# Tiles on SBUF's left side moved 96 bytes against the tiles on its right side

## The chip, the cores and the metric

The kernel runs on one core of a Trainium2 chip. The core has a matrix engine (TensorE, PE in the profile, whose weight loads have a row of their own, PEld), a vector engine (DVE), a scalar engine (ACT), GpSimd (POOL), a queue engine that issues transfers (SP), and 16 DMA engines that move data between DRAM and the on-chip memory SBUF. SBUF has 128 partitions; a tile takes the same byte range in each of them, and "address" below means the byte offset within a partition. The metric is the time of one execution in microseconds on the device, taken as the median of several runs.

## What is computed

One residual block on 512 tokens of width 1024, all in float32. The reference, cut to its shape:

```python
h = rms_norm(x, norm1_g)
proj = h @ w_in          # q,k,v of branch A | q,k,v of branch B | gates gA, gB
out_a = chunked_attention(qa, ka, va, q_norm_g, k_norm_g, rel_bias)  # 8 heads x 64
out_b = stick_breaking_attention(qb, kb, vb)                         # 8 heads x 64
mixed = sigmoid(gA) * (out_a @ w_branch_a) + sigmoid(gB) * (out_b @ w_branch_b)
x = x + mixed @ w_out
hid = causal_conv3(rms_norm(x, norm2_g) @ w_ffn_up) + conv_b         # 2 x 2816 wide
x = x + (silu(hid[gate]) * hid[up]) @ w_ffn_down
```

## The kernel before

Every float32 product is made of three TensorE products. A number is split into a high part that TensorE takes exactly (`hi`, type fp32r) and the rest (`lo`), and `mm3` issues hi*hi, hi*lo and lo*hi into one PSUM bank. ACT makes the high part by a copy, DVE the low part by a subtraction. The activations after each norm are kept so in two tiles, `hth` and `htl` (128 x 8 x 512). The weights come from DRAM in chunks of 128 x 2048 into `raw`, and are split into `whi` and `wlo`, two buffers of each.

A matmul has two operands in SBUF. The stationary one (128 x 128) is loaded into the array by a weight load (PEld); the moving one (128 x 256 or 128 x 512) is streamed past it. The weight load of the next matmul runs beside the matmul before it. In a row of the profile such as `pg<-hth,whi_up 128x512` the two tiles stand behind the arrow, in the order of the names or not; the text says which is which.

The stages in order of time, and the operands of their matmuls:

- 0 to about 53 us: `uA`, `vA` (L433, L439): `hth`/`htl` stationary, `whi`/`wlo` moving, mostly 512 wide.
- 50 to 315 us: the two attentions, with fill-in projections between their steps: `qA`, `kA`, `vB` (`hth`/`htl` stationary, weights moving, 256 wide), `gA`, `qkB`, `gB` (weights stationary, `hth`/`htl` moving, 512 wide), `yA` (weights stationary, attention outputs `oh`/`ol` moving, 512 wide).
- 315 to 382 us: `yB` and the output projection `wo` (weights with attention outputs, or with `mh`/`ml`), then the second norm, which writes `hth`/`htl` anew.
- 382 to 612 us: the up projection. `up0`, `up1` 256 wide and the plain `up` chunks 512 wide have weights stationary and `hth`/`htl` moving (L300 to L302). Twelve chunks use a seven-product scheme (L1169), 256 wide: three of its seven products move `hth`/`htl`, four move sums of them, `ts`.
- 612 to 722 us: the down projection (L1269): the pair tiles `ax`, `ay` are stationary, `whi_dn`/`wlo_dn` moving, 512 wide.

SBUF is filled from two ends. The pools made without `side="right"` grow from the low end: `sm` (the parameters' tile `par`), `wp` (`raw`, `whi`, `wlo`), and then the pools of the attention stages (`cp`, `pv`, `pst`, `pqn`, `ppt`, `pwk`, `po`, `pc`, `ppk`), which later give their place to the pool `fp` of the feed-forward part. The pool `hp` (side="right") holds `hth` and `htl` at the high end; for the down projection `hp2` takes its place and holds `ax9`, `ay9`, `ax10`, `ay10`, one `raw` and two `t2` tiles.

The addresses that the built program gives to some of these tiles, with the remainder by 64 and by 256:

| tile | pool, side | address | mod 64 | mod 256 |
|---|---|---|---|---|
| par | sm, left | 1152 | 0 | 128 |
| whi, wlo (two each) | wp, left | 18304, 26752, 35200, 43648 | 0 | 128 |
| v (first) | pv, left | 68480 | 0 | 128 |
| ax1 | fp, left | 68480 | 0 | 128 |
| wxh | fp, left | 126848 | 0 | 128 |
| ts1 | fp, left | 139648 | 0 | 128 |
| w2l (later also one `ax`) | fp, left | 180608 | 0 | 128 |
| oh (first) | po, left | 164736 | 0 | 128 |
| hth | hp, right | 196576 | 32 | 224 |
| htl | hp, right | 212960 | 32 | 224 |
| ay9, ax10 | hp2, right | 208864, 215008 | 32 | 224 |

The matmuls cut their operands at columns that are multiples of 128, so at multiples of 512 bytes. Three kinds of chunk begin later in their buffer, by the variable `sh` (in columns of 4 bytes) of `split_gen`: `qA`, `kA`, `vB` by 48 columns (192 bytes), and `up0`, `up1` and the twelve seven-product chunks by 16 (64 bytes), whose other weight tiles `wxh`, `wxl`, `w2h`, `w2l` also begin 16 columns in. So on the left every operand that the projections give to TensorE lies on a multiple of 64 bytes, and on the right each lies 32 bytes past one.

The order on each engine is that of a scheduler with a timeline model, which sorts the program by priorities; the code around the change is `norm1` (one call per block of 128 tokens: ACT squares and sums into `ss`, DVE and POOL turn it into the scale columns `cols`) and `norm_T`, the second norm's counterpart.

Of the kernel before, what the change touches and what calls it, by code (L numbers as in the profile page):

```python
# [8 lines left out]
F32 = mybir.dt.float32  # L9
# [6 lines left out]
P = 128  # L16
# [58 lines left out]
def block_kernel(ctx: ExitStack, tc: tile.TileContext, x, xt, params, g2, rbx, wts, wd0, wd1, out):  # L75
# [6 lines left out]
    sm = ctx.enter_context(tc.tile_pool(name="sm", bufs=1))  # L82
# [5 lines left out]
    def apool(name):  # L88
        return ap_ctx.enter_context(tc.tile_pool(name=name, bufs=1))
# [2 lines left out]
        apool(n) for n in ("pv", "pst", "pqn", "ppt", "pwk", "po")]  # L92
    pool_c = apool("pc")
    pool_pk = apool("ppk")
    par = sm.tile([P, 192], F32, tag="par", name="par")
    A.dma_start(par[:, 0:8], params[:, 0:8])
    A.preload_act_table_set("exp_and_others")
    WARM = 9
# [8 lines left out]
    def rstd_of(ss, n, width, name):  # L107

        r = pool_c.tile([P, 8], F32, tag="rs", name=name, bufs=4)
        V.tensor_scalar(r[:, :n], ss, 1.0 / width, EPS, op0=ALU.mult, op1=ALU.add)  # L110
        G.tensor_tensor(r[:, :n], r[:, :n], nhalf[:, :n], op=ALU.pow)
        return r
# [241 lines left out]

    def norm_T(src, xn, gain, t, psum, nm):

        ss = pool_c.tile([P, 1], F32, tag="ss", name=f"ss_{nm}{t}", bufs=4)
        dump = pool_st.tile([P, D], F32, tag="skh", name=f"dump_{nm}{t}", bufs=2)
        A.activation(dump, src, AF.Square, accum_out=ss)
        rs = rstd_of(ss, 1, D, f"rs_{nm}{t}")  # L360
        for b in range(2):
            cs = slice(b * 512, (b + 1) * 512)
            V.scalar_tensor_tensor(xn[:, cs], src[:, cs], rs[:, 0:1], gain[b], op0=ALU.mult, op1=ALU.mult)
            ps = psum(f"tp_{nm}{t}{b}")
            for k in range(4):
                PE.transpose(ps[:, k * P:(k + 1) * P], xn[:, (4 * b + k) * P:(4 * b + k + 1) * P], ident)
            p3 = ps.rearrange("p (k q) -> p k q", k=4)
            hv = hth[:, 4 * b:4 * b + 4, t * P:(t + 1) * P]
            A.copy(hv, p3)
            V.tensor_tensor(htl[:, 4 * b:4 * b + 4, t * P:(t + 1) * P], p3, hv.bitcast(F32), op=ALU.subtract)  # L370

            xf = pool_wk.tile([P, S], F32, tag="wa", name=f"xf_{nm}{t}{b}", bufs=5)
            A.copy(xf, ps)
            G.dma_start(htd[t, b], xf)
# [16 lines left out]

    def norm1(t):
        c = slice(t, t + 1)
        ss = pool_c.tile([P, 1], F32, tag="ss", name=f"ss1{t}", bufs=4)
        dump = pool_st.tile([P, D], F32, tag="skh", name=f"dump1{t}", bufs=2)
        A.activation(dump, xtok[t], AF.Square, accum_out=ss)
        V.tensor_scalar(ss, ss, 1.0 / D, EPS, op0=ALU.mult, op1=ALU.add)
        G.tensor_tensor(rstd[:, c], ss, nhalf[:, 0:1], op=ALU.pow)
        V.tensor_scalar_mul(epsq[:, c], ss, EPS)
        V.tensor_scalar_mul(nrstd[:, c], rstd[:, c], -1.0)  # L400
# [404 lines left out]
    for t in range(NT):  # L805
        norm1(t)
# [35 lines left out]
    for s in range(len(steps)):  # L842
# [8 lines left out]
        br, h, t, e = pend.pop(0)  # L851
# [85 lines left out]
    def fin_out(t, hf, ps):  # L937
        cs = slice(hf * 512, (hf + 1) * 512)
        V.tensor_tensor(x2[:, t, cs], ps, x2[:, t, cs], op=ALU.add)
        if hf == 1:  # L940
            SP.dma_start(x2d[t], x2[:, t, :])
            if t == 0:
                late["xn"] = pool_qn.tile([P, 2, D], F32, tag="qkn", name="xn2")
            xn = late["xn"][:, t, :] if t < 2 else pool_st.tile([P, D], F32, tag="sq", name=f"xn2{t}", bufs=2)
            norm_T(x2[:, t, :], xn, gb, t, lambda n: BANK(n, t // 2), "n2")
# [404 lines left out]
    ss = {}  # L1350
# [85 lines left out]
```

## Time and profile before

| | before |
|---|---|
| median of 3 runs | 724.76 us (724.34 to 725.47) |
| the profiled execution's own time | 724.38 us |
| span of its instructions | 722.6 us |
| TensorE (PE) busy | 717.1 us, 99% of the span |
| weight loads (PEld) busy | 624.9 us, 86% |
| DVE busy | 589.2 us, 82% |
| ACT busy | 433.1 us, 60% |
| POOL busy | 85.7 us, 12% |
| granted TensorE clock | full in every slice |

The profiled execution lies 0.38 us under the median. Matmuls overlap: the next one starts before the one ahead has ended, so the mean duration of a matmul in a row is longer than the distance from start to start, by some 163 ns. Rows of the same width can still be compared with each other: a matmul that starts its successor later also ends later.

### The profile page before, as it was taken

The page shows a single profiled execution, that of the slowest core. Times are in us where ns is not written, and L with a number is a line of the kernel's source. Part 1 is how long each engine was busy: PE and PEld are TensorE (multiplying, and loading weights), DVE is VectorE, ACT ScalarE, POOL GpSimd, SP SyncE. Part 2 cuts the span into 40 slices and gives each one's busy share as a digit, 9 for nine tenths or more (in the row PEclk, how much of TensorE's full clock was granted, in tenths as well). Part 3 has the DMA queues.
Part 4 walks back from the last instruction along what each step waited for, and adds up shares of the span by engine and source line. Part 5 has one row for each costly group of instructions (what it writes and reads, how often), then busy time and mean ns, then how long its engine had stood idle before and what let it go on. Part 6 is the DMA issues. An engine that isn't in the chain of part 4 may idle for free.

```text
span 722.6 us, 11266 instructions
## 1 busy us (share of the span) xinstructions
PE 717.1 (99%) x4091; PEld 624.9 (86%) x4091; DVE 589.2 (82%) x1049; ACT 433.1 (60%) x803; POOL 85.7 (12%) x123
## 2 busy tenths in 40 slices
PE   9999999999999999999999999999999999999997
PEld 7889998888988888888889989999899988888885
DVE  6668878786999999869467698888787979998686
ACT  7576656667776766534236566668667874544531
POOL 2501200000121211000003002212012111000000
PEclk9999999999999999999999999999999999999999
DMA  8712235444434383685967859999688889674463
GB/s 322 282 72 88 81 124 184 180 161 152 168 133 160 125 297 118 217 268 213 347 236 285 286 207 316 313 315 267 216 221 240 240 229 393 189 262 169 170 214 117
DMA packets 51864, 154.98 MB, mean 214 GB/s; under 512 B 5600, under 2 KB 12384, under 8 KB 44000
## 3 DMA queue, kind: packets, MB, share of 16 engines
q1 hardware_dynamic: 44256, 133.67, 52.3%
q0 software_dynamic: 7264, 20.45, 10.8%
q8 instruction: 32, 0.52, 0.3%
q14 instruction: 24, 0.20, 0.1%
q10 hardware_dynamic: 288, 0.14, 0.1%
HBM read 116.49 MB, written 30.41 MB: 203 GB/s over the span
## 4 chain that ended last, share of the span: by engine, by line
PE 97%; DVE 1%; DMA 1%; SPq 0%; issue 0%; DVEq 0%
PE p L1169 16%; PE P L1269 15%; PE vA L433 3%; PE uA L433 3%; PE pg L302 3%; PE pg L301 3%; PE pg L300 3%; PE pu L302 2%; PE pu L300 2%; PE pu L301 2%; PE gB L301 2%; PE gB L300 2%; PE qkB L301 2%; PE qkB L302 2%; PE qkB L300 2%; PE gB L302 2%
## 5 line engine op out<-in xcount | busy, mean ns | idle before, releaser
L165 ACT CAST whi_dn<-raw_dn 128x1024 fp32r<-128x1024 f32 x33 | 34.4, 1051 | 25.8 <-PE P L1269 10.1
L1269 PE MATMUL P<-whi_dn,ax 128*128 128x512 f32 x144 | 44.8, 391 | 0.0
L161 DVE TENSOR_TENSOR wlo_dn<-raw_dn,whi_dn 128x1024 fp32r<-128x1024 f32 x33 | 40.1, 1223 | 4.8 <-ACT whi_dn L165 4.8
L1269 PE MATMUL P<-whi_dn,ay 128*128 128x512 f32 x132 | 41.0, 391 | 0.0
L744 POOL TENSOR_SCALAR_AFFINE_SELECT bB<-bB 128x128 f32<-128x128 f32 x32 | 21.8, 687 | 146.3 <-DVE bB L743 125.6
L207 DVE TENSOR_TENSOR pkr<-pkr 128x512 f32<-128x512 f32 x40 | 27.4, 685 | 11.2 <-issue 5.5
L1169 PE MATMUL p<-ts,whi_up 128*128 128x256 f32 x192 | 35.1, 278 | 0.0
L302 PE MATMUL pg<-hth,wlo_up 128*128 128x512 f32 (+1 forms) x96 | 34.4, 359 | 0.0
L301 PE MATMUL pg<-htl,whi_up 128*128 128x512 f32 (+1 forms) x96 | 34.4, 358 | 0.0
L300 PE MATMUL pg<-hth,whi_up 128*128 128x512 f32 (+1 forms) x96 | 34.2, 356 | 0.0
L1269 PEld LDWEIGHTS P<-whi_dn,ax 128*128 128x128 f32 x144 | 27.1, 188 | 5.8
L302 PE MATMUL pu<-hth,wlo_up 128*128 128x512 f32 (+1 forms) x90 | 31.9, 355 | 0.0
L301 PE MATMUL pu<-htl,whi_up 128*128 128x512 f32 (+1 forms) x90 | 31.9, 355 | 0.0
L300 PE MATMUL pu<-hth,whi_up 128*128 128x512 f32 (+1 forms) x90 | 31.9, 355 | 0.0
L243 DVE TENSOR_TENSOR wlo_up<-raw_up,whi_up 128x1024 fp32r<-128x1024 f32 x24 | 28.9, 1221 | 1.6 <-ACT whi_up L242 1.6
L1169 PEld LDWEIGHTS p<-ts,whi_up 128*128 128x128 f32 x192 | 29.3, 188 | 0.1
L1269 PEld LDWEIGHTS P<-whi_dn,ay 128*128 128x128 f32 x132 | 24.8, 188 | 5.2
L742 DVE TENSOR_TENSOR_SCAN aB<-aB,reset 128x127 f32<-128x127 f32 (+3 forms) x32 | 25.9, 816 | 3.0 <-ACT aB L737 3.0
L1269 PE MATMUL P<-wlo_dn,ax 128*128 128x512 f32 x72 | 28.1, 391 | 0.0
L1169 PE MATMUL p<-hth,whi_up 128*128 128x256 f32 x96 | 26.9, 280 | 0.0
L1169 PE MATMUL p<-htl,whi_up 128*128 128x256 f32 x96 | 26.9, 280 | 0.0
L1169 PE MATMUL p<-hth,wlo_up 128*128 128x256 f32 x96 | 26.8, 280 | 0.0
(350 smaller groups left out, 2541.0 us busy)
## 6 DMA issues: line engine op xcount, KB each, us to landing
parked<-pkr SPq DMA_DIRECT2D x45, 256.0 KB, 3.1
raw_dn<-in_wd SPq DMA_DIRECT2D x11, 1024.0 KB, 4.9
pkr<-in_wts SPq DMA_DIRECT2D x10, 1024.0 KB, 7.1
raw_up<-in_wts SPq DMA_DIRECT2D x10, 1024.0 KB, 6.5
raw_up<-in_wts SPq DMA_DIRECT2D x12, 512.0 KB, 5.9
raw_dn<-in_wd SPq DMA_DIRECT2D x11, 512.0 KB, 3.3
wxl_up<-parked SPq DMA_DIRECT2D x21, 256.0 KB, 4.6
ayd<-ay POOLq DMA_DIRECT2D x7, 768.0 KB, 5.3
```

The source lines that it names most:

```text
L161: chain("halves", V.tensor_tensor(o, x, y, op=op))
L165: chain("casts", A.copy(hi[:, sl], src))
L207: V.tensor_tensor(b[o], b[x], b[y], op=op)
L243: V.tensor_tensor(l[:, sl], src[:, sl], h[:, sl].bitcast(F32), op=ALU.subtract)
L300: ins = PE.matmul(ps, sh, mh, start=first, stop=False)
L301: PE.matmul(ps, sh, ml, start=False, stop=False)
L302: PE.matmul(ps, sl, mh, start=False, stop=last)
L433: PE.matmul(pss[t], st[:, 4 * half + k, t * P:(t + 1) * P], mv[:, k, :], start=half == 0 and k == 0 and j == 0, stop=half == 1 and k == 3 ...
L742: V.tensor_tensor_scan(ar, ar, reset[:, S - n:S - 1][:, ::-1], 1.0, op0=ALU.mult, op1=ALU.max)
L744: G.affine_select(b[:, n - P:n], b[:, n - P:n], pattern=[[-1, P]], compare_op=ALU.is_gt, fill=0.0, base=0, channel_multiplier=1)
L1169: PE.matmul(ps, st, mv[:, k, :], start=first and k == 0 and n == 0, stop=last and k == 3 and n == 2, skip_group_check=True)
L1269: chain("products", PE.matmul(dst, st, mv, start=first and n == 0, stop=last and n == 2, skip_group_check=True))
```

## The change

The tile `par` gets 216 columns instead of 192, that is 864 bytes instead of 768; its added columns are not used. All that is allocated behind it on the left side begins 96 bytes later. To keep the left side from running into the right one, the small tile `ss` (4 bytes, in a slot of 32) is kept twice instead of four times, in both norms; what lies behind it in the pools `pc` and `ppk` begins 32 bytes later instead of 96. The pools `hp` and `hp2` stay where they are.

```diff
-    par = sm.tile([P, 192], F32, tag="par", name="par")
+    par = sm.tile([P, 216], F32, tag="par", name="par")
@@ norm_T
-        ss = pool_c.tile([P, 1], F32, tag="ss", name=f"ss_{nm}{t}", bufs=4)
+        ss = pool_c.tile([P, 1], F32, tag="ss", name=f"ss_{nm}{t}", bufs=2)
@@ norm1
-        ss = pool_c.tile([P, 1], F32, tag="ss", name=f"ss1{t}", bufs=4)
+        ss = pool_c.tile([P, 1], F32, tag="ss", name=f"ss1{t}", bufs=2)
```

In the built program the left side's tiles of the table behind `par` then lie 32 past a multiple of 64 and 224 past a multiple of 256 (before 0 and 128): the same remainders as those of `hth`, `htl` and `hp2`'s tiles. The instructions and their order are the same on all engines. Only semaphore waits differ, on ACT, in the first norm. The rows of ACT there, with - for before and + for the change (dump and ss are `norm1`'s tiles, the numbers name buffers, and the brackets hold what the instruction waits for):

```order
 L396 ACTIVATE dump_197,ss_196<-xtok_139 128x1024 [waits DMAHW3_49]
 L396 ACTIVATE dump_204,ss_203<-xtok_141 128x1024 [waits DMAHW4_49]
-L396 ACTIVATE dump_211,ss_210<-xtok_143 128x1024 [waits DMAHW5_49,Activation_49]
+L396 ACTIVATE dump_211,ss_210<-xtok_143 128x1024 [waits DVE_49,DMAHW5_49,Activation_49,Pool_49]
 L463 ACTIVATE sq_uA_313<-uA_225 128x512 [waits PE_49]
-L396 ACTIVATE dump_218,ss_217<-xtok_145 128x1024 [waits DMAHW6_49,Activation_49]
+L396 ACTIVATE dump_218,ss_217<-xtok_145 128x1024 [waits DVE_49,DMAHW6_49,Activation_49,Pool_49]
 L463 ACTIVATE sq_uA_337<-uA_226 128x512 [waits PE_49]
```

The third and the fourth `norm1` now wait also until DVE and POOL have read the `ss` of the first and the second, since they write into the same places.

## The prediction

> **What bounds the kernel now.** I read the page's busy times and the chain of waits first, then the waits of TensorE, then its groups of matmuls in stretches in which only one kind of matmul runs. The page:
>
> ```profile
> PE 717.1 (99%) x4091; PEld 624.9 (86%) x4091; DVE 589.2 (82%) x1049; ACT 433.1 (60%) x803; POOL 85.7 (12%) x123
> PE 97%; DVE 1%; DMA 1%; SPq 0%; issue 0%; DVEq 0%
> ```
>
> TensorE is busy in 717.1 of 722.6 us and makes 97% of the chain. The list of waits names TensorE twice, with 1.1 us at the start and
>
> ```profile
> PE gA L300 <- DVE mixA L622: 0.3, 1, 0.3
> ```
>
> So no engine and no transfer holds TensorE up; the time is its matmuls, one behind the other. The change alters neither their number nor their order. What it can alter is how long one matmul takes, and the trace shows that this depends on where its operands lie. Two stretches of the down projection, 640 to 660 us and 662.2 to 671.8 us, by shape:
>
> ```profile
> L1269 PE MATMUL P<-whi_dn,ax 128*128 128x512 f32 x60 | 18.5, 389 | 0.0
> L1269 PE MATMUL P<-wlo_dn,ax 128*128 128x512 f32 x30 | 11.7, 389 | 0.0
> ...
> L1269 PE MATMUL P<-whi_dn,ax 128*128 128x512 f32 x28 | 8.8, 397 | 0.0
> L1269 PE MATMUL P<-wlo_dn,ax 128*128 128x512 f32 x14 | 5.6, 396 | 0.0
> ```
>
> The same line, shape and moving tiles: 389 ns in the one, 396 to 397 in the other. In the first stretch the stationary `ax` tiles are on the left side like the moving ones; in the second they are `ax9` and `ax10` on the right side, 32 bytes out of step by 64. Now the up projection, 407 to 427 us (`hth`/`htl` moving, weights stationary), the first projection, 12 to 20 us (`hth`/`htl` stationary), and a seven-product chunk, 428 to 434 us, 256 wide:
>
> ```profile
> L302 PE MATMUL pg<-hth,wlo_up 128*128 128x512 f32 x16 | 6.4, 399 | 0.0
> L301 PE MATMUL pg<-htl,whi_up 128*128 128x512 f32 x16 | 6.3, 394 | 0.0
> L300 PE MATMUL pg<-hth,whi_up 128*128 128x512 f32 x16 | 6.3, 392 | 0.0
> ...
> L433 PE MATMUL uA<-whi_uA,htl 128*128 128x512 f32 x13 | 4.2, 397 | 0.0
> ...
> L1169 PE MATMUL p<-ts,wxl_up 128*128 128x256 f32 x6 | 1.7, 276 | 0.0
> L1169 PE MATMUL p<-ts,whi_up 128*128 128x256 f32 x8 | 1.4, 276 | 0.0
> L1169 PE MATMUL p<-hth,whi_up 128*128 128x256 f32 x4 | 1.1, 282 | 0.0
> L1169 PE MATMUL p<-htl,whi_up 128*128 128x256 f32 x4 | 1.1, 280 | 0.0
> L1169 PE MATMUL p<-hth,wlo_up 128*128 128x256 f32 x4 | 1.1, 278 | 0.0
> ```
>
> Both operands on the left: 389 (512 wide), 276 (256 wide). One left, one right: 392 to 399, 397, and 278 to 282. It does not matter which of the two is on the right. **The trace has no stretch with both operands displaced alike**, and that is what the change makes of nearly every matmul: left and right then have equal remainders by 64 and by 256. The question of this case is whether a matmul is slow because one operand lies off a multiple of 64, or because its two operands are out of step with each other.
>
> **The change, part by part.** I take the second: out of step. The rows above fit it without exception, and equal sizes for a displaced moving (6 ns) and a displaced stationary operand (8 ns) are what a collision of the two streams would give. Against it: 512 wide a displaced moving operand costs 6 ns and 256 wide 3, as if it paid by the element, while a collision with one weight load should cost the same at both widths. The remainders by 256 are in step too. Before, the fast 512-wide matmuls differ by 0 and the fast 256-wide ones (`ts` against weights 64 bytes further on) by 192, moving minus stationary; after, all 512-wide ones of the projections differ by 0, and `qA`, `kA`, `vB` (192 bytes on, moving) and the up chunks (64 bytes on, stationary) by 192. By this reading each mixed matmul falls to the pace of the left-left ones. Counts from the grouped rows of the whole trace:
>
> ```profile
> L300 PE MATMUL pg<-hth,whi_up 128*128 128x512 f32 x64 | 25.3, 395 | 0.0
> L300 PE MATMUL pu<-hth,whi_up 128*128 128x512 f32 x58 | 22.9, 395 | 0.0
> L1169 PE MATMUL p<-hth,whi_up 128*128 128x256 f32 x96 | 26.9, 280 | 0.0
> L1169 PE MATMUL p<-ts,whi_up 128*128 128x256 f32 x192 | 35.1, 278 | 0.0
> L300 PE MATMUL pg<-hth,whi_up 128*128 128x256 f32 x32 | 8.9, 279 | 0.0
> L433 PE MATMUL vA<-whi_vA,htl 128*128 128x512 f32 x32 | 12.7, 397 | 0.0
> L300 PE MATMUL gA<-hth,whi_gA 128*128 128x512 f32 x64 | 25.6, 400 | 0.3 <-DVE mixA L622 0.3
> L300 PE MATMUL yA<-oh_A,whi_yA 128*128 128x512 f32 x32 | 12.9, 402 | 0.0
> L300 PE MATMUL vB<-whi_vB,hth 128*128 128x256 f32 x64 | 18.4, 287 | 0.0
> L302 PE MATMUL kA<-whi_kA,htl 128*128 128x256 f32 x32 | 9.1, 284 | 0.0
> L439 PE MATMUL uA<-wlo_uA,hth 128*128 128x256 f32 x8 | 1.3, 281 | 0.0
> ```
>
> Each row stands for three (hi*hi, hi*lo, lo*hi).
> - Up projection, 512 wide: 3 x (64 + 58) and 18 of the held ones, 384 matmuls, mean 395 less 389: 384 x 6 ns = 2.3 us.
> - Seven-product chunks, `hth`/`htl` moving: 3 x (96 + 28 + 20) = 432, by 280 less 277: 1.3 us.
> - `up0`, `up1`: 6 x 32 = 192, by 279 less 276: 0.6 us.
> - `uA`, `vA`: 84 + 96 = 180, by 397 less 389: 1.4 us.
> - `gA`, `qkB`, `gB`: 9 x 64 = 576. These run between attention steps, and there `yA`, with both operands on the left, takes 402, no less than `gA`'s 400. So the bounds are 0 and 6 ns each; `yA`'s short groups are broken up more often than these, so I take the value nearer to the clean stretches, 4: 2.3 us (0 to 3.5).
> - `qA`, `kA`, `vB`: 2 x 96 + 192 = 384, 282 to 291 ns. Bounds 0, by the same doubt, and 9 (286 less 277); I take 4, near the 281 less 277 of `uA`'s first matmuls before any attention: 1.5 us (0 to 3.5).
> - Down projection with `ax9`, `ax10`, `ay9`, `ay10`: 84, by 397 less 389: 0.7 us.
>
> Sum 10.1 us, with the two bounds 6.3 to 13.3. The transposes stay.
>
> What can take some of it back is an engine that now keeps up:
>
> ```profile
> 182.00:315.00 133.00, 133.00 (x706) 113.14 (x705) 120.79 (x216) 87.37 (x188) 21.24 (x30) 1.00 0.51 180
> 406.00:612.00 206.00, 206.00 (x1396) 188.68 (x1396) 175.26 (x269) 141.22 (x235) 33.99 (x44) 1.00 0.88 272
> ```
>
> (Columns: PE, PEld, DVE, ACT, POOL busy, clock, DMA share.) DVE is busy in 120.8 of the 133 us of branch B's attention, and the DMA engines in 88% of the up projection. Taking 2 us out of the first and 4 out of the second leaves both under their limits on the mean; for local waits, of which there are none now, I take off 1 us, between 0 and, if DVE set the pace of that whole stage, the 2 us it gains. **Net 9.1 us.**
>
> At nothing: the wider `par` (the same columns are loaded), and DVE's and ACT's own work, of which this pair, into the right side and within the left, is alike:
>
> ```profile
> L370 DVE TENSOR_TENSOR htl<-tp_n,hth 128x512 fp32r<-128x512 f32 x8 | 5.1, 684 | 1.5 <-ACT hth L369 1.5
> L276 DVE TENSOR_TENSOR wlo_wo<-raw_wo,whi_wo 128x512 fp32r<-128x512 f32 x16 | 10.1, 685 | 4.2 <-ACT whi_wo L271 4.2
> ```
>
> The new waits of ACT cost nothing as well. The third and fourth squares wait for POOL's reads of the first and second `ss`, and those are over (18.65 and 19.92) when ACT comes to them (19.29 and 22.16); were they not, `uA`'s squares would stand behind them on ACT.
>
> ```profile
> 18.09 0.56 POOL L398 TENSOR_TENSOR cols<-ss,nhalf 128x1 f32<-128x1 f32 x1 [13.43 <-DVE ss L397]
> 19.36 0.56 POOL L398 TENSOR_TENSOR cols<-ss,nhalf 128x1 f32<-128x1 f32 x1 [0.72 <-DVE ss L397]
> ...
> 19.29 1.06 ACT L396 ACTIVATE dump<-xtok 128x1024 f32<-128x1024 f32 x1 [0.19 <-DMA xtok<-in_x]
> ...
> 22.16 1.05 ACT L396 ACTIVATE dump<-xtok 128x1024 f32<-128x1024 f32 x1
> ```
>
> Transfers into tiles off a multiple of 64 are bounded by 0 and by what is hidden: no row shows TensorE waiting for one, so a slower landing costs nothing until the slack of a chunk is used up; I take 0.
>
> The profiled execution took 724.38 us; less 9.1 that is 715.3, and with the 0.38 us by which the median lies above it, **715.6 us**.
>
> **The rivals.**
>
> *Each operand pays for its own place.* A read that begins 32 bytes past a multiple of 64 is slow, whatever the other does; both displaced cost no more than one, because the next matmul waits for the later of two streams. Then the mixed matmuls stay as they are and the left-left ones join them: 378 of the down projection, 192 of `wo`, 96 of `yB`, 666 x 8 ns = 5.3 us, and the 576 with `ts` by 3 to 4.5 ns, 2.2 us. That is 7.5 us more, 732.3 us: slower. For it stands the payment by the element noted above; it decides if pairs displaced alike run at 397 and 280. If the two costs add, mixed ones rise too: 384 x 8, 576 x 8, 624 x 4, 180 x 6, 384 x 3 and 84 x 6 ns make 12.9 us, the left-left ones pay 5.7 more, with the 7.5 in all 26.1 us, 750.9 us. Against both: nothing but simplicity.
>
> [...]
>
> *The place is the side, not the remainder.* Every slow row has one operand at the high end of SBUF. If it is the region that costs, or what else goes on in those stages, a shift of 96 bytes changes nothing: 724.8 us. Against it: left tiles from 18304 to 180608 all run at one pace in the down projection, so distance alone does nothing.
>
> [...]
>
> **How the numbers follow.** Out of step, in full or in part (a part being only the clean stretches, 6.3 us, 718.5): 0.73. No change: 0.10. Each for itself, the dearer of the two: 0.13, and added: 0.04. The likeliest gives 715.6 us, its own range 711.5 (13.3 us off) to 719. The range that takes in the unchanged case, and the slower one in its mildest form, a third of its 7.5 us, goes to 727: **711.5 to 727**. Chances: faster 0.73, within 0.2% (about what a measurement of this kernel can tell from no change) 0.10, slower 0.17.
>
> **What would show it.** Right: the 512-wide matmuls of the up and the first projection at 389 to 391 ns, those on `ax9` no slower than those on other `ax`, 256-wide rows with `hth` and with `ts` equal at 276 to 278; TensorE's busy time about 9 us less, without new waits beyond 1 us. Wrong: `wo`, `yB` and the down projection above 395 ns, or all rows as before; or matmuls that shrink while TensorE waits for DVE or a load.

## The result, and the profile after

The changed kernel takes 717.79 us (median of 4 runs, 717.17 to 718.89) against 724.90 us before (4 runs): 7.1 us less, a ratio of 0.9904 with a 95% interval of 0.9886 to 0.9921. The forecast was 715.6 us, with a range of 711.5 to 727. The profiled execution took 718.12 us, its span is 716.4. The page's busy times after, and then the list of TensorE's waits (microseconds in all, times, the longest):

```profile
PE 709.9 (99%) x4091; PEld 623.6 (87%) x4091; DVE 589.0 (82%) x1049; ACT 432.2 (60%) x803; POOL 85.7 (12%) x123
```

```profile
PE warm L352 <- DVE warm L349: 1.1, 1, 1.1
PE p L1169 <- DVE wlo_up L243: 0.8, 1, 0.8
PE gA L300 <- DVE mixA L622: 0.3, 1, 0.3
```

TensorE's busy time fell by 7.2 us (717.1 before) with the same 4091 matmuls, and DVE's, ACT's and POOL's stayed within 1 us. A weight load in the projections takes 188 ns in the median of every stage, before and after; what changes is the time from one matmul to the next (for `gA` 233.5 ns before and 228.6 after, on the mean of unbroken runs). The span fell by 6.2 us, since TensorE now stands idle 1.0 us longer, 0.8 of it in one wait for a split on DVE that it did not have before.

The same stages as in the prediction, in the profile after, by shape: the up projection (402 to 421 us), the first projection (12 to 20 us), and the down projection on `ax9` and `ax10` (657 to 666 us):

```profile
L302 PE MATMUL pg<-hth,wlo_up 128*128 128x512 f32 x16 | 6.2, 389 | 0.0
L300 PE MATMUL pg<-hth,whi_up 128*128 128x512 f32 x15 | 5.8, 389 | 0.0
...
L433 PE MATMUL uA<-whi_uA,htl 128*128 128x512 f32 x13 | 4.1, 389 | 0.0
...
L1269 PE MATMUL P<-whi_dn,ax 128*128 128x512 f32 x27 | 8.4, 389 | 0.0
L1269 PE MATMUL P<-wlo_dn,ax 128*128 128x512 f32 x14 | 5.4, 389 | 0.0
```

All are at 389 ns, where 392 to 399, 397 and 396 to 397 stood before. Every operand there now lies 32 bytes past a multiple of 64, so the place itself is not what cost those 3 to 10 ns. The 256-wide rows of the seven-product chunks did not all follow. Chunk 10 (484.2 to 490 us) and chunks 13 and 14 (516 to 530 us), after:

```profile
L1169 PE MATMUL p<-ts,wxh_up 128*128 128x256 f32 x16 | 2.8, 276 | 0.0
L1169 PE MATMUL p<-hth,whi_up 128*128 128x256 f32 x4 | 1.1, 278 | 0.0
...
L1169 PE MATMUL p<-ts,whi_up 128*128 128x256 f32 x24 | 4.4, 281 | 0.0
L1169 PE MATMUL p<-hth,wlo_up 128*128 128x256 f32 x12 | 3.4, 281 | 0.0
L1169 PE MATMUL p<-ts,wxh_up 128*128 128x256 f32 x11 | 2.1, 281 | 0.0
```

In chunk 10 products with `hth` and with `ts` run at 276 to 278 ns; in chunks 13 and 14 both run at 281, with operands at the same remainders by 256. Before, the rows with `ts` had 276 to 277 in the prediction's stretch and 277 to 278 over the whole trace.

Below, "pace" is the distance from the start of one matmul to that of the next, worked out from the start times in the trace as the mean over runs of one kind and width, without steps over 260 ns (512 wide) or 140 ns (256 wide), in which something else came between. "Distance" is the address of the moving operand less that of the stationary operand loaded beside it (that of the next matmul), modulo 256. The four buffers `whi` and `wlo` lie 8448 bytes apart, 33 times 256, so that by 512 two of them differ from the other two. In the changed kernel the down projection takes all four in turn and runs at 226.7 ns on each, so the period is not 512.

### The profile page after: what moved, and what is told of

Its sections match the earlier page's. It is cut to its first block, busy times and chain, and to the rows that moved or that the text cites. A ratio compares the mean times of both kernels' runs of the same rounds, so it can differ in the third digit from the quotient of the medians.

```text
span 716.4 us, 11264 instructions
## 1 busy us (share of the span) xinstructions
PE 709.9 (99%) x4091; PEld 623.6 (87%) x4091; DVE 589.0 (82%) x1049; ACT 432.2 (60%) x803; POOL 85.7 (12%) x123
## 4 chain that ended last, share of the span: by engine, by line
PE 92%; DVE 3%; DMA 3%; SPq 1%; ACT 0%; issue 0%; POOL 0%; DVEq 0%
PE p L1169 16%; PE P L1269 15%; PE vA L433 3%; PE uA L433 3%; PE gB L300 2%; PE gB L301 2%; PE qkB L302 2%; PE gB L302 2%; PE qkB L300 2%; PE qkB L301 2%; PE wo L300 2%; PE wo L301 2%; PE wo L302 2%; PE gA L300 2%; PE pg L300 2%; PE pg L301 2%
## 5 line engine op out<-in xcount | busy, mean ns | idle before, releaser
L1269 PE MATMUL P<-whi_dn,ax 128*128 128x512 f32 x144 | 44.4, 389 | 0.0
L1269 PE MATMUL P<-whi_dn,ay 128*128 128x512 f32 x132 | 40.8, 389 | 0.0
L1169 PE MATMUL p<-ts,whi_up 128*128 128x256 f32 x192 | 35.5, 279 | 0.0
L302 PE MATMUL pg<-hth,wlo_up 128*128 128x512 f32 (+1 forms) x96 | 34.0, 354 | 0.0
L300 PE MATMUL pg<-hth,whi_up 128*128 128x512 f32 (+1 forms) x96 | 33.9, 353 | 0.0
L1269 PEld LDWEIGHTS P<-whi_dn,ax 128*128 128x128 f32 x144 | 27.0, 188 | 5.6
L300 PE MATMUL pu<-hth,whi_up 128*128 128x512 f32 (+1 forms) x90 | 31.5, 350 | 0.0
L302 PE MATMUL pu<-hth,wlo_up 128*128 128x512 f32 (+1 forms) x90 | 31.5, 349 | 0.0
L1169 PEld LDWEIGHTS p<-ts,whi_up 128*128 128x128 f32 x192 | 29.6, 189 | 0.1
L1269 PEld LDWEIGHTS P<-whi_dn,ay 128*128 128x128 f32 x132 | 24.8, 188 | 5.1
L1269 PE MATMUL P<-wlo_dn,ax 128*128 128x512 f32 x72 | 28.0, 389 | 0.0
L1169 PE MATMUL p<-ts,wlo_up 128*128 128x256 f32 x96 | 26.9, 280 | 0.8 <-DVE wlo_up L243 0.8
L276 DVE TENSOR_TENSOR wlo_up<-raw_up,whi_up 128x1024 fp32r<-128x1024 f32 (+1 forms) x26 | 24.6, 973 | 2.9 <-ACT whi_up L271 2.8
L1169 PE MATMUL p<-hth,whi_up 128*128 128x256 f32 x96 | 26.8, 279 | 0.0
```

The source lines that it names most:

```text
L276: V.tensor_tensor(lo[:, sl], raw[:, sl], hi[:, sl].bitcast(F32), op=ALU.subtract)
L300: ins = PE.matmul(ps, sh, mh, start=first, stop=False)
L302: PE.matmul(ps, sl, mh, start=False, stop=last)
L1169: PE.matmul(ps, st, mv[:, k, :], start=first and k == 0 and n == 0, stop=last and k == 3 and n == 2, skip_group_check=True)
L1269: chain("products", PE.matmul(dst, st, mv, start=first and n == 0, stop=last and n == 2, skip_group_check=True))
```

## The experiments

The theory on record: a matmul is slow when its two operands are out of step with each other. Its rivals: each operand pays for its own place; the side of SBUF, or any move of the left side, is what counts.

**The right side moved instead.** From the kernel before:

```diff
+    rp = ctx.enter_context(tc.tile_pool(name="rp", bufs=1, side="right"))
+    rp.tile([P, 24], F32, tag="edge", name="edge")
     hp = h_ctx.enter_context(tc.tile_pool(name="hp", bufs=1, side="right"))
@@ both norms
-        ss = pool_c.tile([P, 1], F32, tag="ss", ..., bufs=4)
+        ss = pool_c.tile([P, 1], F32, tag="ss", ..., bufs=2)
```

> The right side is moved 96 bytes down instead of the left side 96 up: every operand of the projections then lies on a multiple of 64 bytes, and left and right are in step by 256. In step is all that counts: the same as the change, 717 to 719 us, 512-wide rows of the up projection at 389 to 391 ns. Each operand pays for its own place (what is left of that theory, the 256-wide matmuls at 116 to 118 ns from start to start after the change instead of 113): 2 us faster than the change, about 716 us, with the seven-product rows at 276 to 277 ns.

Measured: 718.19 us (717.52 to 718.56), ratio to before 0.9906 (0.9892 to 0.9919). Three groups over the whole trace, of the changed kernel and then of this one; the two added lines make L300 and L1169 of the other kernels L302 and L1171:

```profile
L300 PE MATMUL pu<-hth,whi_up 128*128 128x512 f32 x58 | 22.6, 389 | 0.0
L300 PE MATMUL pg<-hth,whi_up 128*128 128x512 f32 x64 | 25.0, 391 | 0.0
L1169 PE MATMUL p<-ts,wxh_up 128*128 128x256 f32 x112 | 20.7, 279 | 0.0
```

```profile
L302 PE MATMUL pu<-hth,whi_up 128*128 128x512 f32 x58 | 22.6, 389 | 0.0
L302 PE MATMUL pg<-hth,whi_up 128*128 128x512 f32 x64 | 25.0, 391 | 0.0
L1171 PE MATMUL p<-ts,wxh_up 128*128 128x256 f32 x112 | 20.7, 279 | 0.0
```

The rows are the same (389, 391, 279), here with every projection operand on a multiple of 64. So the gain does not hang on which side moves, nor on multiples of 64. The 256-wide loss is here too (279, and 281 in the late chunks), so it is no price of a place either: that expectation of the rival, 716 us, failed. The changed kernel, whose tiles on both sides lie off a multiple of 64, is no slower than this one (717.79 and 718.19 us), so that place costs the transfers nothing that shows in the time.

**A third of the way, from either side.** The right side down by 32 bytes (as above with 8 columns, `ss` four times), or the left side up by 32:

```diff
-    par = sm.tile([P, 192], F32, tag="par", name="par")
+    par = sm.tile([P, 200], F32, tag="par", name="par")
```

> The right side is moved down by 32 bytes only: every operand lies on a multiple of 64, but left and right differ by 64 when taken by 128 or 256. If being in step by 64 is enough: 716 to 719 us. If it takes a step of 128 or 256 bytes: the projections with one operand on each side stay slow, 722 to 725 us, with the up projection's 512-wide rows at 395 ns.

> The left side is moved up by 32 bytes instead of 96, and the small tile ss keeps its four places: all operands 32 bytes past a multiple of 64, left and right differ by 64 when taken by 128 or 256. In step by 64 is enough: 717 to 719 us. Own place: all rows slow, 732 us. A step of 128 or 256 needed: 722 to 725 us.

Measured: right side 722.16 us (722.06 to 722.85), ratio 0.9966 (0.9952 to 0.9979); left side 722.77 us (722.17 to 723.19), ratio 0.9969 (0.9958 to 0.9981). In the one all operands lie on multiples of 64, in the other all 32 bytes past one; the distances are the same in both. Rows of the first (right side), then of the second:

```profile
L304 PE MATMUL pg<-hth,wlo_up 128*128 128x512 f32 x64 | 25.1, 393 | 0.0
L435 PE MATMUL uA<-whi_uA,htl 128*128 128x512 f32 x28 | 9.6, 395 | 0.0
L302 PE MATMUL pg<-hth,whi_up 128*128 128x256 f32 x32 | 9.0, 283 | 0.0
```

```profile
L302 PE MATMUL pg<-hth,wlo_up 128*128 128x512 f32 x64 | 25.1, 393 | 0.0
L433 PE MATMUL uA<-whi_uA,htl 128*128 128x512 f32 x28 | 9.6, 396 | 0.0
L300 PE MATMUL pg<-hth,whi_up 128*128 128x256 f32 x32 | 9.0, 283 | 0.0
```

The two kernels agree within 1 ns in these rows, and in the pace of every projection but for the first 24 matmuls (117.7 and 115.1 ns, at distance 192), though no operand has the same place modulo 64: the place is out, the distance stays. And being in step by 64 is not enough: the up projection's 512-wide matmuls (distance 64) have a pace of 229.0 ns, nearly the 227 of distance 0, but `uA` (distance 192) still has 233.3, and the 256-wide `up0`, `up1` (distance 0) have 119.8 instead of 117.1 before.

**The left side moved by 64**, with `ss` twice (`par` of 208 columns).

> The left side is moved up by 64 bytes, with ss twice: left on multiples of 64, right 32 past one, as before the change. In step by 64: as slow as before, 724 to 726 us, rows with hth at 392 to 399 ns. If any move of the left side or the ss edit had brought the gain: 717 to 719 us.

Measured: 725.86 us (725.54 to 726.37), ratio 1.0009 (1.0001 to 1.0018): no gain. So neither moving the left side as such nor the smaller `ss` does it. Two of its groups over the whole trace:

```profile
L300 PE MATMUL pg<-hth,whi_up 128*128 128x512 f32 x64 | 25.3, 395 | 0.0
L1169 PE MATMUL p<-ts,whi_up 128*128 128x256 f32 x192 | 35.7, 280 | 0.0
```

The up projection's distance is 32 here, where it was 96 before. In the seven-product chunks the products with `hth` and `htl` are at distance 224 and those with `ts` still at 192, as before the change; yet the `ts` ones have a mean pace of 116.6 ns instead of 114.2.

**The whole curve in one kernel.** From the changed kernel, each chunk of the up and the down projection begins at its own place in its weight buffer (the columns stand in a table by chunk):

```diff
+SHIFT = {f"dn0_{i}": n for i, n in enumerate((0, 4, 8, 12, 16, 20, 24, 28, 32, 36, 40))}
+SHIFT |= {f"dn1_{i}": n for i, n in enumerate((44, 48, 52, 56, 60, 64, 2, 6, 1, 10, 0))}
...
+        sh = SHIFT.get(key, sh)
```

> From the changed kernel; every chunk of the up and the down projection begins at another place in its weight buffer, 0 to 256 bytes on, so that each shows the pace at one distance of its moving from its stationary operand. If only the distance modulo 256 counts: 0 and 256 bytes at 227 ns from start to start (512 wide), 64 bytes with the weights stationary near 229, 96, 160, 192 and 224 at 233 to 234, as on the earlier runs; places between, at 4 to 48 bytes, are new, and a slow climb from 227 within the first 32 bytes or a step at one of them shows the grain of it. 256 wide: 192 (moving less stationary) at 113 or 118, 0 at 119 to 120, 96 and 128 at 118 to 120. If something else than the distance counts, a chunk at the same distance as before will not show the same pace.

Measured in one run: 723.90 us beside 724.89 before. Four chunks of its down projection, at 0, 32, 64 and 4 bytes (L1269 is L1274 here):

```profile
L1274 PE MATMUL P<-whi_dn,ax0b 128*128 128x512 f32 x14 | 4.3, 389 | 0.0
...
L1274 PE MATMUL P<-whi_dn,ax 128*128 128x512 f32 x14 | 4.4, 395 | 0.0
...
L1274 PE MATMUL P<-whi_dn,ax 128*128 128x512 f32 x14 | 4.3, 392 | 0.0
...
L1274 PE MATMUL P<-whi_dn,ay 128*128 128x512 f32 x10 | 3.2, 399 | 0.0
```

The pace by distance, in ns, over all chunks of this run (512 wide in the down projection where there is one, 256 wide in the seven-product chunks):

| distance, bytes | 0 | 4 | 16 | 32 | 64 | 80 | 96 | 128 | 160 | 192 | 224 | 240 |
|---|---|---|---|---|---|---|---|---|---|---|---|---|
| 512 wide | 227 | 236 | 231 | 233 | 229.5 | 231 | 234 | 233 | 234 | 233 | 233 | 227 or 233 |
| 256 wide | 119.8 | | 120 | 117 | 118 | | 120 | 119 | 118 | 113 or 118 | 118 | 118 |

The distances that the other kernels have (0, 32, 64, 96, 128, 160, 192, 224) show their pace here too, to about 1 ns, in other stages and with either operand on either side. One column of 4 bytes off is the worst place measured for 512 columns, 236 ns, and 16 bytes off has 231: there is no slow climb. At 240 bytes the down projection ran at 227 and the up projection at 233: two paces at one distance. The chunk at 256 bytes (distance 0 again) began at 224 to 236 ns for eight matmuls and then fell to 227 and stayed: this stream at distance 0 did not have the good pace from its first matmul. So the expectation that the distance alone sets the pace held for most distances and failed at these.

**Distance 0 for the 256-wide matmuls.** The changed kernel with all chunks at the start of their buffers:

```diff
-        sh = 48 if key[:2] in ("qA", "kA", "vB") else 16 if key in ("up0", "up1") or is_seven(i) else 0
+        sh = 0
@@ fetch_extra
-        ... [:, 16:1552] ...
+        ... [:, 0:1536] ...
```

> The changed kernel with all chunks at the start of their buffers: the 256-wide matmuls of qA, kA, vB, of up0, up1 and of the seven-product chunks then have distance 0 instead of 192 by 256. If the pace goes by the distance and by the width: they run at 119 to 120 ns from start to start instead of 113 to 118: 1008 x 3.5 + 192 x 5 + 384 x 3.7 ns = 5.9 us more than the change, 723 to 724 us. If being in step is the best place at every width: no slower than the change, 714 to 718 us.

Measured: 723.00 us (722.74 to 723.71), ratio 0.9974 (0.9964 to 0.9984), 5.2 us above the changed kernel, with the 256-wide pace at 119.1 to 120.0 in all projections and the 512-wide ones unchanged. Two of its groups, 512 and 256 wide:

```profile
L300 PE MATMUL pg<-hth,whi_up 128*128 128x512 f32 x64 | 25.0, 391 | 0.0
L1169 PE MATMUL p<-ts,wxh_up 128*128 128x256 f32 x112 | 21.3, 283 | 0.0
```

In step is best 512 wide (227 ns in the table) and among the worst 256 wide (119.8).

**Why the late chunks lag.** In the changed kernel the pace at distance 192 is either 113.3 or 117.8 ns for a dozen matmuls or more on end, and from 505 us on it is 117.8. This kernel puts other matmuls between them:

```diff
@@ fetch_extra
+        o = 56 if j in SUMS else 16
-        ... [:, 16:1552] ...
+        ... [:, o:o + 1536] ...
```

> The changed kernel, but in the seven chunks whose second weight tiles are split late (11, 13, 14, 16, 17, 18, 20) those tiles begin 56 columns into their buffer instead of 16: their 36 matmuls of a chunk have distance 32 by 256, the other 48 keep 192. In these chunks of the changed kernel all 84 ran at 117.8 ns from start to start, while at the same distance in earlier chunks they ran at 113.3. If the pace at distance 192 is a state that is carried from matmul to matmul and that a few matmuls at another distance break: the 36 run at 117, the 48 at 113 to 114, in all 7 x 84 x 2.7 ns = 1.6 us less than the change, 716.2 us. If something else slows those late chunks (other engines, transfers): the 48 stay at 117.8 and the time stays at 717.8.

> The changed kernel itself once more, for a time beside the others: 717 to 719 us, and if the pace of the seven-product chunks is not chance, again 113.3 ns in chunk 10 and 117.8 ns in chunks 13 to 20.

Measured: 716.57 us (716.06 to 716.92), ratio to before 0.9879 (0.9864 to 0.9894); the changed kernel beside it 717.91 us (717.16 to 719.35), so 1.3 us less, without overlap of the runs. Chunks 13 and 14 again, 515 to 530 us (one line was added: L1169 is L1170):

```profile
L1170 PE MATMUL p<-ts,whi_up 128*128 128x256 f32 x24 | 4.2, 276 | 0.0
L1170 PE MATMUL p<-hth,wlo_up 128*128 128x256 f32 x12 | 3.3, 277 | 0.0
L1170 PE MATMUL p<-ts,wxh_up 128*128 128x256 f32 x11 | 2.1, 279 | 0.0
L1170 PE MATMUL p<-hth,wxh_up 128*128 128x256 f32 x4 | 1.1, 279 | 0.0
```

The rows on `whi` and `wlo`, of which nothing was changed, went from 281 to 276 and 277; those on `wxh` to 279, the level of their new distance 32. In the seven chunks the pace of the unchanged matmuls is 115.0 and of the moved ones 116.9 ns, against 117.4 for both in the changed kernel (a part of chunk 11, up to 499 us, ran at 113.4 there, which the expectation overlooks). Other engines and transfers had the same work to do, so it is not they that held these chunks at 117.4: only the distance of the matmuls between was changed, and the unchanged ones went to 115.0. The matmuls at distance 32 do not always break the slow pace: the unchanged ones ran at 113.7 ns in chunk 17 and still at 116.8 in chunk 20, where 113 to 114 was expected. Nor does any other distance do: with 224 between them, in the kernel moved by 64, the `ts` products had 116.6. The changed kernel's second profile shows again 113.3 in chunk 10 and 117.8 in chunks 13 to 20, but at 460 us, after the start of chunk 8, it left the fast pace and kept 117.8 ns to 473 us, where the first profile has 113.3 until 470. It left it just after the one wait that its list shows for these chunks:

```profile
PE p L1169 <- DMA w2l_up<-parked: 0.2, 1, 0.2
```

The first profile's wait of 0.8 us, at 429 us, was followed by the fast pace again within six matmuls. So of two breaks in the stream the one of 0.2 us was followed by 117.8 ns and the one of 0.8 us by 113.3. What selects the pace, there and at a turn from 512 to 256 columns, is open.

## Why the prediction was right, and where it was off

The bound, the cause and the sign were right: time of the matmuls themselves (TensorE busy 717.1 us before, 709.9 after), which goes by the two operands' distance. "In step" is its right name for the 512-wide ones alone, and by 256 bytes, not by 64 (227 ns at distance 0, 229.0 and 233.3 at 64 and 192). At 256 columns distance 0 is slow (119.1 to 120.0 ns), and the gain there rests on the 192 that the prediction had read from the `ts` rows. The terms, as forecast and as measured (matmuls in unbroken runs by the change of their pace, profile before to profile after):

| term | forecast, us | measured, us |
|---|---|---|
| up projection, 512 wide | 2.3 | 2.2 |
| `gA`, `qkB`, `gB` | 2.3 (0 to 3.5) | 2.6 |
| `uA`, `vA` | 1.4 | 1.1 |
| `qA`, `kA`, `vB` | 1.5 (0 to 3.5) | 1.2 |
| `up0`, `up1` | 0.6 | 0.4 |
| `ax9`, `ax10`, `ay9`, `ay10` | 0.7 | 0.6 |
| seven products with `hth`/`htl` | 1.3 | 0.4 |
| seven products with `ts` | 0 | -0.9 |
| sum | 10.1 | 7.6 |
| taken back by waits | 1.0 | 1.0 (span less busy time) |

The step that failed is "each mixed matmul falls to the pace of the left-left ones", for the seven-product chunks alone: 1.8 of the 2.5 us that the sum was too high. The distance 192 was read from the `ts` rows as a pace; it is one of two seen at this distance, 113.3 and 117.8 ns. Before the change the products with `hth` and `htl`, at distance 32, came between those with `ts`: the first three with `ts` after them had 118.3, 119.9 and 116.3 ns to the next matmul on the mean, those from the fourth on 113 to 113.6, so the fast pace was entered anew each time. With all at 192 the means at the same places are 116.0 to 116.4, and from 505 us on nothing broke the 117.8. The kernel that puts a distance of 32 between them brings 1.3 us back, so this account is shown for that part; why the slow pace outlasted the breaks in some chunks is not.

The bounds on the attention stages held, and the doubt behind them was not needed: 228.6 ns for `gA` and 229.5 for `yA` once both are in step, so `yA`'s 402 ns in the row, unchanged by the edit, came with the breaks between its matmuls: at 9 of the 96 the next one starts 285 to 318 ns later, and these 9 take 470 ns on the mean, the others 392. That the waits came to what was taken off is luck: one wait for DVE in the up projection rather than several in the attention, and in the second profile of the changed kernel it is gone.

The argument held against the theory, payment by the element, compared unlike things: 6 ns at 512 columns belong to distance 96 and 3 ns at 256 columns to distance 32. At the same distance of 96 the surcharge over the best pace is 6.8 ns (233.6 less 226.8) and 6.4 ns (119.7 less 113.3), nearly the same per matmul at both widths, which is what the prediction expected of a collision with one weight load. But at other distances the two widths part: 6 and 3.7 ns at 32, 2.7 and 4.5 at 64, none and 6.5 at 0. So neither a price per element nor one price per collision fits them all, and whether anything collides inside the chip no run here shows.

The rivals are settled: own place by the two kernels with equal rows and all operands on or off multiples of 64; the side and the `ss` edit by the move of 64 bytes, 725.86 us, and by the gain when the right side moved instead, 718.19 us. A distance of 16 bytes cost 4 to 5 ns at 512 columns, and one of 64 bytes 2 to 3. In the kernel with the whole curve only the stationary operand of the up projection is moved, and the pace of its 512-wide matmuls goes between 229 and 234 ns.

## What to carry to other kernels

Where TensorE is the bound, compare the mean duration of matmuls of one shape between stages: here a spread of 2 to 3% at full clock and without waits (397 to 399 against 389 ns) came from the SBUF addresses of the moving and the stationary operand taken together, and moving one side by 96 bytes was a cheap test (724.90 to 717.79 us). In this kernel 512-wide fp32r matmuls ran best with the same address modulo 256 for both (227 ns), 256-wide ones with 192 bytes between them (moving less stationary, 113.3 ns), and the second kind has a slow pace (117.8 ns) that matmuls at distance 32 broke in most of the chunks here (115.0 ns on the mean), and those at distance 224 did not reliably (116.6). A forecast from rows should ask in what company those rows ran: in the changed kernel one distance had 113.3 ns in chunk 10 and 117.8 in chunks 13 to 20, each kept from matmul to matmul.

## What the runs showed of the hardware that was not expected

- In the kernel with the whole curve the pace of a 512-wide fp32r matmul is 227 ns at distance 0, 229 to 231 at 16, 64, 80 and 112, and 232 to 236 at the others but for 240 bytes; 4 bytes are enough for 236.
- 256 wide, distance 0 is among the slowest there, 119.8 ns, and 192 the only one measured in any kernel here at which 113.3 was kept.
- At distance 192 (256 wide) and 240 (512 wide) two paces were seen, 113.3 and 117.8, 227 and 233; a stream kept the one it was in over a dozen matmuls or more and several tiles (117.8 in chunks 13 to 20 of the changed kernel). At distance 0 (512 wide) a stream took six to eight matmuls at 224 to 236 ns before it ran at 227: after another distance in the kernel with the whole curve, and after two breaks in the changed kernel, at 612 and at 705 us.
